# The causal mask of a hybrid decoder layer: added on VectorE instead of multiplied in on TensorE, with a re-set table of waits

## The chip, the cores and the metric

The kernel runs on one core of a Trainium2 chip. The metric is the device time of one execution in microseconds (us), the median of several; lower is better. TensorE (PE) multiplies matrices into the eight PSUM banks, VectorE (DVE) and ScalarE (ACT) work on 128 partitions at a time and can read and write banks, GpSimd (POOL) does a few small operations, and DMA queues bring the weights from memory. Each engine takes its instructions in the order in which the program issues them, and waits at an instruction whose inputs are not there.

## What is computed

One decoder layer on 256 tokens of width 1024. An input projection feeds two groups of heads: eight heads of softmax attention (width 64, rotary on 16 dimensions) and four heads of retention (rotary queries and keys, a fixed decay table in place of a softmax, normalising and a gate). Both go through an output projection; then come cross-attention into 256 memory rows and a gated feed-forward part, each with normalising before and after and a residual.

The attention blocks are 256 keys long and the sequence has 256 tokens, so only a query's own block counts, and the reference comes down to causal attention:

```python
    scale = dh ** -0.5
    ...
        s_own = jnp.einsum('bhqd,bhld->bhql', qb, k_own).astype(jnp.float32) * scale
        own_pos = cur * L + key_offsets
        s_own = jnp.where(own_pos[None, :] <= q_pos[:, None], s_own, NEG_INF)
        ...
        p = jax.nn.softmax(logits, axis=-1)
```

The mask is what the change concerns: keys later than the query get -1e30 before the softmax.

## The kernel before

**The main line.** All large products are cut into 257 steps (`steps`), each of six or so products of 128x128 weights on 512 columns; PE runs them one after the other. Weights arrive as raw 128x1024 blocks and are split into a high and a low part, one ScalarE copy (L196) and one VectorE subtraction (L197) each; three products then stand in for one of full precision. Steps 0 to 16 make q and k, 17 to 24 the retention's q and k, 25 to 32 its values, 33 to 40 its gate, 41 to 48 the attention's values, and 49 to 64 the output projection. Step 49 starts with the gated retention rows of the first 128 tokens, step 50 with those of the last 128.

**The side work.** Everything else (rotations, softmax, retention, normalising) is written as generators. A generator does some work, yields a number of steps, and is resumed after that many steps (`spawn`, `run_side`); inside a step the side work is issued after the step's products. The numbers come from the table `WAIT`, so the table sets the order of the instructions on every engine. A generator that yields 0 goes on in the same step; one that is spawned by another generator is resumed at the next step at the earliest.

**The splits.** At the end of a step at most one weight is split. Weight `q` may be split at step `i` if `q <= 2 + WAIT["pace"] * 0.01 * i`, if a buffer is free, and if the step had no side work or the weight is near its use (six weights ahead).

**Attention.** `moba_qk` scales q or k (L241), turns it (L278 to L283), and after `rope_*` steps transposes it through the one bank of pool C (L287, L288). `mq` is the wait ahead of q's. `moba_units` then runs three softmax units through `moba_unit` and `softmax_unit`: m00 (first 128 queries, all heads, 128 keys), m10 and m11 (last 128 queries, 256 keys, four heads each). A unit fills two of the four banks of pool S with scores (`fill`, L352); the mask is added by a product of an identity with the mask table: after the scores with bfloat16 operands in m00 and m10 (L356), ahead of them with float32r operands in m11 (L345). Then VectorE takes the maxima (L302), ScalarE the exponentials (L312), VectorE normalises (L315, L317), and after `nm_*` steps PE transposes the weights (L325) into two banks of pool S, which ScalarE (L330) and VectorE (L332) copy out. `u1` and `u2` are the steps between units. In m11, `fill` also issues the first half of the retention scores (`ret_scores`: L423 on PE, L430 on VectorE), and the second half is a generator of its own, `rs` steps later.

**Around it.** `ret_qk` turns and transposes the retention's q and k (L400 to L411). `mem_stats` takes the mean square of the memory rows, their power -1/2 on GpSimd (L219), and `mrow` steps later `row_rms` spreads them over a row through the bank of pool C (L248, L249). `ret_out` and `ret_gate` (`gate0`, `gate1`; transposes L466, split L235, L236) and `moba_pv` (`pv1`; L388) make the operands of the output projection. `x_stats` makes the four operands of the mask products (L1034 to L1037).

By the table before, the steps after which these are issued are: m00's scores 20 and transposes 25; m10's scores 28 and transposes 34; m11's scores and the first retention scores 36, its normalising 40 and transposes 46; retention rotation transposes 27 and 33; the memory row 30; the gates' transposes 42 and 46; the attention-value product 50.

Of the kernel before, what the change touches and what calls it, by code (L numbers as in the profile page):

```python
# [8 lines left out]
F32R = mybir.dt.float32r  # L9
BF16 = mybir.dt.bfloat16  # L10
AF = mybir.ActivationFunctionType
ALU = mybir.AluOpType
AX = mybir.AxisListType

P = 128
# [21 lines left out]

WAIT = {
    "cpb0": 2, "cpb1": 1, "cpv0": 7, "cpv1": 1, "cu0": 3, "cu1": 4, "ex_c0": 2, "ex_c1": 1, "ex_m00": 0,
    "ex_m10": 0, "ex_m11": 4, "f0_0": 8, "f0_1": 5, "g_add": 1, "g_silu": 5, "gate0": 3, "gate1": 6,  # L40
    "gp1": 5, "gp2": 0, "k_add": 0, "k_hl": 3, "lag": 2, "ret": 9, "low": 6, "mq": 0, "mrow": 4, "ms": 21, "mst": 5,
# [5 lines left out]
}  # L47
# [4 lines left out]
C_ID, C_MASK, C_MCOS, C_MSIN, C_RCOS, C_RSIN, C_DEC, C_END = 0, 128, 256, 288, 320, 448, 576, 1600  # L52
# [3 lines left out]
def tile_hybrid_layer(  # L56
# [14 lines left out]
    nc = tc.nc  # L71
    ctx.enter_context(tc.manual_schedule())

    cpool = ctx.enter_context(tc.tile_pool(name="cpool", bufs=1))
# [12 lines left out]
    def tok(t):  # L87
        return slice(t * P, (t + 1) * P)
# [4 lines left out]
    def small(name):  # L93
        return sm.tile([P, 8], F32, tag="sm", name=name)
# [10 lines left out]
    cst = cpool.tile([P, C_DEC], F32, tag="cst", name="cst")  # L105
    xg = cpool.tile([P, 288], F32, tag="xg", name="xg")
    gp = xg[:, 0:32].rearrange("p (g k) -> p g k", g=4)
    x_sb = cpool.tile([P, 2, D], F32, tag="x", name="x_sb")
    identb = cpool.tile([P, P], BF16, tag="identb", name="identb")
    maskb = cpool.tile([P, P], BF16, tag="maskb", name="maskb")  # L110
    identr = cpool.tile([P, P], F32R, tag="identr", name="identr")
    maskr = cpool.tile([P, P], F32R, tag="maskr", name="maskr")
    junk = cpool.tile([P, D], BF16, tag="junk", name="junk")
    mhalf = cpool.tile([P, 8], F32, tag="mhalf", name="mhalf")
    ident = cst[:, C_ID:C_ID + P]
# [5 lines left out]
    T = {}  # L121
# [3 lines left out]
    def need(*keys):  # L125

        missing = [k for k in keys if k not in emitted]
        assert not missing, missing
# [83 lines left out]
    def inv_rms(key, ss0, ss1=None, n=1):  # L212
        v = small(f"v_{key}")
        if ss1 is None:
            nc.vector.tensor_scalar(v[:, :n], ss0, EPS, None, op0=ALU.add)
        else:
            nc.vector.tensor_scalar(v[:, :n], ss0, ss1, EPS, op0=ALU.add, op1=ALU.add)
        r = cpool.tile([P, 8], F32, tag=f"r_{key}", name=f"r_{key}")
        nc.gpsimd.tensor_tensor(out=r[:, :n], in0=v[:, :n], in1=mhalf[:, :n], op=ALU.pow)  # L219
        rstd[key] = r  # L220
        return r

    def mean_square(dst, src, n):
        nc.scalar.activation(junk[:, :n], src, AF.Square, scale=1.0 / 32.0, accum_out=dst)
# [31 lines left out]
    def spawn(gen, wait=0):  # L256
        active.append([step_no[0] + wait, gen])
# [76 lines left out]
    def moba_unit(t, g):  # L334
        keys = P * (t + 1)
        n = D // keys
        hn = n // 2

        def fill(s):

            need(f"q{t}", *[f"k{u}" for u in range(t + 1)])

            ahead = g == 1
            for e in range(2) if ahead else ():
                nc.tensor.matmul(s[e].rearrange("p (h k) -> p h k", h=hn)[:, :, keys - P:keys], identr,  # L345
                                 maskr[:, None, :].to_broadcast([P, hn, P]), start=True, stop=False,
                                 skip_group_check=True)
            for i in range(hn):
                j = g * hn + i
                for e in range(2):  # L350
                    rows = slice(64 * e, 64 * e + 64)
                    nc.tensor.matmul(s[e][:, i * keys:(i + 1) * keys], T["qT"][rows, j, tok(t)],  # L352
                                     T["kT"][rows, j, 0:keys], start=(i == 0 and not ahead),
                                     stop=(ahead and i == hn - 1), skip_group_check=True)
            for e in range(2) if not ahead else ():
                nc.tensor.matmul(s[e].rearrange("p (h k) -> p h k", h=hn)[:, :, keys - P:keys], identb,  # L356
                                 maskb[:, None, :].to_broadcast([P, hn, P]), start=False, stop=True,
                                 skip_group_check=True)
            if ahead:
                scores = ret_scores()  # L360
                spawn(scores, next(scores))
            yield 0

        return softmax_unit(f"m{t}{g}", n, keys, 0.125, fill)

    def moba_units():
# [47 lines left out]
    def ret_scores():  # L414

        need("rqk0", "rqk1")
        for kb in range(2):
            n = P * (2 - kb)
            s = [accS(f"rs{kb}{e}") for e in range(2)]
            for j in range(2):  # L420
                for e in range(2):
                    rows = slice(64 * e, 64 * e + 64)
                    nc.tensor.matmul(s[e][:, j * n:(j + 1) * n], T["rkT"][rows, j, tok(kb)],  # L423
                                     T["rqT"][rows, j, kb * P:256], start=True, stop=True)
            for e in range(2):
                if kb == 0 or e == 0:
                    buf = tmp2k(f"ra{kb}{e}")
                a = buf[:, kb * e * 256:kb * e * 256 + 2 * n].rearrange("p (j i) -> p j i", j=2)
                T[f"ra{kb}{e}"] = a
                nc.vector.tensor_tensor(out=a, in0=s[e][:, 0:2 * n].rearrange("p (j i) -> p j i", j=2),  # L430
                                        in1=T["decay"].rearrange("p (j e) i -> p e j i", e=2)[:, e, :, 0:n], op=ALU.mult)
            if kb == 0:
                yield WAIT["rs"]
# [478 lines left out]
    for what in USE:  # L912
# [4 lines left out]
        elif what[0] == "d":  # L917
            k = int(what[1:])
# [17 lines left out]
    for q, item in enumerate(items):  # L936
        if item[0] == "w":
            continue
        kind, w, g, home, part, plus = item[:6]
# [91 lines left out]
        yield 0  # L1031

    def x_stats():
        nc.vector.tensor_copy(identb, ident)  # L1034
        nc.vector.tensor_copy(maskb, cst[:, C_MASK:C_MASK + P])
        nc.vector.tensor_copy(identr, ident)
        nc.vector.tensor_copy(maskr, cst[:, C_MASK:C_MASK + P])  # L1037
        for t in range(2):
            ss = small(f"ss_x{t}")
            mean_square(ss[:, 0:1], x_sb[:, t, :], D)  # L1040
            inv_rms(f"x{t}", ss[:, 0:1])
        yield 0
# [25 lines left out]
    x_split(2, 3)  # L1068
    opening = {4: lambda: x_split(4, 5), 7: lambda: x_split(6, 7)}
    late = {WAIT["xd"]: x_load, WAIT["xs"]: x_stats, WAIT["ms"]: mem_stats}  # L1070
    pending_split = list(range(2, NQ))

    accs, downs = {}, {}
    for i, s in enumerate(steps):
# [17 lines left out]
        if s[0] == "first":  # L1092
# [3 lines left out]
            h = hls[q][:, :, c * 512:(c + 1) * 512]  # L1096
# [6 lines left out]
        elif s[0] == "col":  # L1103
# [4 lines left out]
            h = hls[q].rearrange("p s (k n) -> p s k n", k=2)  # L1108
            for kk in range(2):
                k = 2 * kp + kk  # L1110
# [9 lines left out]
        elif s[0] == "row":  # L1120
# [13 lines left out]
            for k, w in ops:  # L1134
                begin = half == 0 and (k, w) == ops[0]
                end = half == 1 and (k, w) == ops[-1]
                if w:
                    nc.tensor.matmul(acc, hls[q][:, 0, k * P:(k + 1) * P], T[f"{st}_k"][:, k, :], start=begin, stop=end,  # L1138
                                     skip_group_check=True)
                else:  # L1140
                    nc.tensor.matmul(acc[:, 0:256], hls[q][:, 1, k * P:(k + 1) * P], T[st][:, 0, k, :], start=begin,  # L1141
                                     stop=end, skip_group_check=True)
            if half == 1:
                spawn(done(nt, acc))
        elif s[0] == "down":
            _, q, t, j, kk, halves = s
# [17 lines left out]
        elif s[0] == "seven":  # L1164
            _, q, g, m, part, name, begin = s
# [3 lines left out]
            h = hls[q].rearrange("p s (k n) -> p s k n", k=2)  # L1169
            for kk in range(2):  # L1170
                xh, xl = token_operand(m, 2 * part + kk)
                end = part == 1 and kk == 1
                for n, (a, w) in enumerate(((xh, 0), (xh, 1), (xl, 0))):
                    nc.tensor.matmul(acc, a, h[:, w, kk, :], start=begin and kk == 0 and n == 0, stop=end and n == 2,  # L1174
                                     skip_group_check=True)
# [132 lines left out]
```

## Time and profile before

| | |
|---|---|
| median of 3 runs | 398.38 us (398.0 to 398.8) |
| profiled execution | 400.7 us |
| its span, first to last instruction | 398.9 us |
| PE busy | 390.0 us, 98% |
| VectorE busy | 320.3 us, 80% |
| ScalarE busy | 257.6 us, 65% |
| GpSimd busy | 33.4 us, 8% |
| granted TensorE clock | 0.998 |

Rows of a timeline read: start in us, duration in us, engine, line, operation, output<-inputs, output shape and type<-input shape and type, how many were merged; in brackets the idle time of the engine ahead of it and what ended it. PE is the products, PEld the loading of their weights. A row in the chain of waits has start, duration, engine and line. The ends of products are modelled, so the starts of the next ones are the better mark. In a table of stretches each engine has its busy time and its number of instructions; the last three columns are the granted clock, the share of the DMA engines and GB/s.

### The profile page before, as it was taken

The page shows a single profiled execution, that of the slowest core. Times are in us where ns is not written, and L with a number is a line of the kernel's source. Part 1 is how long each engine was busy: PE and PEld are TensorE (multiplying, and loading weights), DVE is VectorE, ACT ScalarE, POOL GpSimd, SP SyncE. Part 2 cuts the span into 40 slices and gives each one's busy share as a digit, 9 for nine tenths or more (in the row PEclk, how much of TensorE's full clock was granted, in tenths as well). Part 3 has the DMA queues.
Part 4 walks back from the last instruction along what each step waited for, and adds up shares of the span by engine and source line. Part 5 has one row for each costly group of instructions (what it writes and reads, how often), then busy time and mean ns, then how long its engine had stood idle before and what let it go on. Part 6 is the DMA issues. An engine that isn't in the chain of part 4 may idle for free.

```text
span 398.9 us, 5470 instructions
## 1 busy us (share of the span) xinstructions
PE 390.0 (98%) x1969; PEld 323.9 (81%) x1969; DVE 320.3 (80%) x447; ACT 257.6 (65%) x431; POOL 33.4 (8%) x53
## 2 busy tenths in 40 slices
PE   7999999999999999999999999999999999999993
PEld 3888887888888888888888888888887888888882
DVE  3876877586869987677576699999899899999964
ACT  4885973964757865494547766766748685656741
POOL 0010020200011000000001001013113103101000
PEclk9999999999999999999999999999999999999999
DMA  8998837367547676607271459778939878954102
GB/s 275 414 354 268 300 118 252 107 187 287 168 152 223 200 215 204 214 4 235 79 263 55 158 193 358 242 157 315 278 72 279 241 242 175 372 191 71 38 0 105
DMA packets 23067, 80.36 MB, mean 201 GB/s; under 512 B 2560, under 2 KB 3200, under 8 KB 23040
## 3 DMA queue, kind: packets, MB, share of 16 engines
q1 hardware_dynamic: 18288, 62.97, 45.7%
q0 software_dynamic: 4608, 16.78, 17.1%
q8 instruction: 15, 0.25, 0.3%
q10 hardware_dynamic: 144, 0.26, 0.2%
q14 instruction: 12, 0.10, 0.1%
HBM read 78.95 MB, written 1.05 MB: 201 GB/s over the span
## 4 chain that ended last, share of the span: by engine, by line
PE 78%; issue 7%; DMA 7%; DVE 4%; ACT 1%; POOL 1%; SPq 0%; DVEq 0%; ACTq 0%; POOLq 0%
PE acc L1114 11%; PE acc L1116 11%; PE acc L1115 11%; PE acc L1138 7%; PE x L1174 7%; PE acc L1141 4%; PE down L1161 3%; PE down L1159 3%; PE down L1160 3%; PE y L1174 3%; DMA sum_qv<-in_weights_dram 3%; DVE hl L197 2%; PE acc L1102 2%; DMA sum_ret<-in_weights_dram 2%; DMA xr<-in_gx_dram 2%
## 5 line engine op out<-in xcount | busy, mean ns | idle before, releaser
L197 DVE TENSOR_TENSOR hl<-raw,hl 128x1024 fp32r<-128x1024 f32 (+1 forms) x102 | 119.3, 1189 | 16.9 <-ACT hl L196 16.8
L196 ACT ACTIVATE hl<-raw 128x1024 fp32r<-128x1024 f32 (+1 forms) x102 | 102.5, 1031 | 1.1 <-DMA raw<-in_weights_dram 0.9
L196 ACT ACTIVATE hl<-sum_qv 128x1024 fp32r<-128x1024 f32 x22 | 23.0, 1057 | 16.5 <-DVE sum_qv L203 12.9
L1114 PE MATMUL acc<-hl,xT 128*128 128x512 f32 x80 | 32.9, 411 | 0.0
L1159 PE MATMUL down<-hl,fT 128*128 128x512 f32 x80 | 31.3, 392 | 0.0
L1116 PE MATMUL acc<-hl,xT 128*128 128x512 f32 x80 | 31.3, 391 | 0.0
L1115 PE MATMUL acc<-hl,xT 128*128 128x512 f32 x80 | 31.2, 391 | 0.0
L1161 PE MATMUL down<-hl,fT 128*128 128x512 f32 x80 | 31.2, 390 | 0.0
L1160 PE MATMUL down<-hl,fT 128*128 128x512 f32 x80 | 31.1, 389 | 0.0
L197 DVE TENSOR_TENSOR hl<-sum_kT,hl 128x1024 fp32r<-128x1024 f32 x24 | 29.1, 1221 | 1.4 <-ACT hl L196 1.2
L196 ACT ACTIVATE hl<-sum_kT 128x1024 fp32r<-128x1024 f32 x24 | 24.8, 1051 | 5.5 <-DVE sum_kT L203 3.5
L197 DVE TENSOR_TENSOR hl<-sum_qv,hl 128x1024 fp32r<-128x1024 f32 x22 | 26.7, 1219 | 1.9 <-ACT hl L196 1.9
L1174 PE MATMUL x<-hl,comb 128*128 128x512 f32 x96 | 23.6, 392 | 0.4 <-DVE hl L197 0.4
L1174 PE MATMUL x<-hl,x2T 128*128 128x512 f32 x96 | 23.1, 392 | 0.0
L1174 PE MATMUL y<-hl,comb 128*128 128x512 f32 x96 | 23.1, 389 | 0.0
L1174 PEld LDWEIGHTS x<-hl,comb 128*128 128x128 f32 x96 | 17.9, 188 | 4.8 <-DVE hl L197 1.1
L1174 PEld LDWEIGHTS y<-hl,comb 128*128 128x128 f32 x96 | 18.0, 188 | 3.8
L1174 PEld LDWEIGHTS x<-hl,x2T 128*128 128x128 f32 x96 | 17.8, 188 | 3.6
L1161 PEld LDWEIGHTS down<-hl,fT 128*128 128x128 f32 x80 | 15.0, 188 | 3.3 <-DVE fT L664 0.2
L1116 PEld LDWEIGHTS acc<-hl,xT 128*128 128x128 f32 x80 | 15.0, 188 | 3.3
L1114 PEld LDWEIGHTS acc<-hl,xT 128*128 128x128 f32 x80 | 15.0, 188 | 3.2 <-issue 0.3
L1160 PEld LDWEIGHTS down<-hl,fT 128*128 128x128 f32 x80 | 15.0, 188 | 3.1
(260 smaller groups left out, 861.8 us busy)
## 6 DMA issues: line engine op xcount, KB each, us to landing
raw<-in_weights_dram SPq DMA_DIRECT2D x98, 512.0 KB, 4.8
sum_kT<-in_weights_dram POOLq DMA_DIRECT2D x14, 512.0 KB, 6.9
sum_qv<-in_weights_dram POOLq DMA_DIRECT2D x10, 512.0 KB, 5.7
sum_ret<-in_weights_dram POOLq DMA_DIRECT2D x8, 512.0 KB, 4.8
gpost<-in_gpost_dram SPq DMA_DIRECT2D x3, 512.0 KB, 5.2
x_sb<-in_x_dram SPq DMA_DIRECT2D x2, 512.0 KB, 8.1
memn<-in_mem_dram SPq DMA_DIRECT2D x2, 512.0 KB, 8.0
mr<-in_memT_dram SPq DMA_DIRECT2D x2, 512.0 KB, 7.4
```

Source lines behind the costliest of these rows:

```text
L196: nc.scalar.activation(h[:, 0, n], raw[:, n], AF.Copy)
L197: nc.vector.tensor_tensor(out=h[:, 1, n], in0=raw[:, n], in1=h[:, 0, n].bitcast(F32), op=ALU.subtract)
L1102: nc.tensor.matmul(accs[(c, t)], T["xT"][:, hx, q, tok(t)], h[:, hw, :], start=begin, stop=False)
L1114: nc.tensor.matmul(acc, xh, h[:, 0, kk, :], start=(first and kk == 0), stop=False)
L1115: nc.tensor.matmul(acc, xh, h[:, 1, kk, :], start=False, stop=False)
L1116: nc.tensor.matmul(acc, xl, h[:, 0, kk, :], start=False, stop=(last and kk == 1))
L1138: nc.tensor.matmul(acc, hls[q][:, 0, k * P:(k + 1) * P], T[f"{st}_k"][:, k, :], start=begin, stop=end, skip_group_check=True)
L1141: nc.tensor.matmul(acc[:, 0:256], hls[q][:, 1, k * P:(k + 1) * P], T[st][:, 0, k, :], start=begin, stop=end, skip_group_check=True)
L1159: nc.tensor.matmul(acc, fh, wh, start=first, stop=False, skip_group_check=True)
L1160: nc.tensor.matmul(acc, fh, wl, start=False, stop=False, skip_group_check=True)
L1161: nc.tensor.matmul(acc, fl, wh, start=False, stop=last, skip_group_check=True)
L1174: nc.tensor.matmul(acc, a, h[:, w, kk, :], start=begin and kk == 0 and n == 0, stop=end and n == 2, skip_group_check=True)
```

## The change

The mask products go, and after the scores of each unit VectorE adds the mask table to the diagonal 128 keys of every head, in the bank, one instruction for each of the unit's two banks. m11 has the same order as the others. The four operand copies in `x_stats` and their tiles go. In the table of waits ten entries change:

| entry | before | after |
|---|---|---|
| `mq`, ahead of q's rotation | 0 | 3 |
| `rope_q0`, `rope_q1`, rotation of q to its transposes | 5, 8 | 2, 5 |
| `u2`, from m10's transposes to m11's scores | 2 | 0 |
| `nm_m11`, normalising to transposes | 6 | 4 |
| `rs`, between the halves of the retention scores | 0 | 1 |
| `gate0`, `gate1` | 3, 6 | 7, 8 |
| `pv1`, ahead of the attention-value product | 2 | 3 |
| `pace`, of the weight splits | 58 | 59 |

```diff
@@ moba_unit, fill
-            ahead = g == 1
-            for e in range(2) if ahead else ():
-                nc.tensor.matmul(s[e].rearrange("p (h k) -> p h k", h=hn)[:, :, keys - P:keys], identr,
-                                 maskr[:, None, :].to_broadcast([P, hn, P]), start=True, stop=False,
-                                 skip_group_check=True)
             for i in range(hn):
...
                     nc.tensor.matmul(s[e][:, i * keys:(i + 1) * keys], T["qT"][rows, j, tok(t)],
-                                     T["kT"][rows, j, 0:keys], start=(i == 0 and not ahead),
-                                     stop=(ahead and i == hn - 1), skip_group_check=True)
-            for e in range(2) if not ahead else ():
-                nc.tensor.matmul(s[e].rearrange("p (h k) -> p h k", h=hn)[:, :, keys - P:keys], identb,
-                                 maskb[:, None, :].to_broadcast([P, hn, P]), start=False, stop=True,
-                                 skip_group_check=True)
-            if ahead:
+                                     T["kT"][rows, j, 0:keys], start=(i == 0), stop=(i == hn - 1), skip_group_check=True)
+            for e in range(2):
+                diag = s[e].rearrange("p (h k) -> p h k", h=hn)[:, :, keys - P:keys]
+                nc.vector.tensor_tensor(out=diag, in0=diag, in1=cst[:, None, C_MASK:C_MASK + P].to_broadcast([P, hn, P]),
+                                        op=ALU.add)
+            if g == 1:
                 scores = ret_scores()
                 spawn(scores, next(scores))
@@ x_stats
-        nc.vector.tensor_copy(identb, ident)
-        nc.vector.tensor_copy(maskb, cst[:, C_MASK:C_MASK + P])
-        nc.vector.tensor_copy(identr, ident)
-        nc.vector.tensor_copy(maskr, cst[:, C_MASK:C_MASK + P])
```

By the new table, m11's scores and the first retention scores are issued after step 34, in the step of m10's transposes; m11's normalising after step 38 and its transposes after 42; the gates' transposes after steps 46 and 48; the attention-value product after 51. The other steps named above stay.

More of the change, by code (lines that the diff above doesn't have):

```diff
@@ L39 @@
     "cpb0": 2, "cpb1": 1, "cpv0": 7, "cpv1": 1, "cu0": 3, "cu1": 4, "ex_c0": 2, "ex_c1": 1, "ex_m00": 0,
-    "ex_m10": 0, "ex_m11": 4, "f0_0": 8, "f0_1": 5, "g_add": 1, "g_silu": 5, "gate0": 3, "gate1": 6,
-    "gp1": 5, "gp2": 0, "k_add": 0, "k_hl": 3, "lag": 2, "ret": 9, "low": 6, "mq": 0, "mrow": 4, "ms": 21, "mst": 5,
[3 rows of a table removed]
+    "ex_m10": 0, "ex_m11": 4, "f0_0": 8, "f0_1": 5, "g_add": 1, "g_silu": 5, "gate0": 7, "gate1": 8,
+    "gp1": 5, "gp2": 0, "k_add": 0, "k_hl": 3, "lag": 2, "ret": 9, "low": 6, "mq": 3, "mrow": 4, "ms": 21, "mst": 5,
[3 rows of a table added]
     "xa_mix0": 8, "xa_mix1": 4, "near": 18, "now": 5, "sum": 3, "ts": 2, "ts0": 1, "ts1": 3, "s_silu": 4, "s_t0": 4, "s_mul": 1, "s_t1": 1, "xd": 3, "xh_cross0": 1, "xh_cross1": 1, "xh_mix0": 2, "xh_mix1": 2, "xn0": 2, "xn1": 2, "hold0": 1, "hold": 2, "hold_low": 3,
@@ L108, in tile_hybrid_layer @@
     x_sb = cpool.tile([P, 2, D], F32, tag="x", name="x_sb")
[L109 to L112, printed above, removed]
     junk = cpool.tile([P, D], BF16, tag="junk", name="junk")
```

6 rows, old and new, of the table WAIT are left out of this document.

## The prediction

> **What bounds the kernel now.** I read the page first, then the table of waits for the tensor engine (PE), then the busy time by stretches, then the timeline from 22 to 96 us engine by engine, and last the chain of waits. The page gives the span, the waits give what PE ever waited for:
>
> ```profile
> span 398.9 us, 5470 instructions
> ```
> ```profile
> PE acc L1102 <- ACT hl L196: 1.4, 1, 1.4
> ...
> PE x L1174 <- DVE hl L197: 0.4, 1, 0.4
> ```
>
> PE waits at the very start and once late, and nowhere between, so a microsecond of PE work taken out or a microsecond of new PE waiting moves the end by about itself. The profiled execution took 400.7 us, 1.8 of it around the span and 2.3 more than the median of the runs, 398.38 us; I work in differences inside the span and put them on the median. The change sits in the attention part, and there the two helper engines are not idle (columns: PE, PEld, DVE, ACT, POOL busy us):
>
> ```profile
> 40.00:50.00 10.00, 10.00 (x54) 8.10 (x54) 8.84 (x14) 9.25 (x19) 0.00 (x0) 1.00 0.82 297
> 50.00:60.00 10.00, 10.00 (x53) 8.00 (x52) 7.24 (x12) 7.45 (x19) 2.04 (x2) 1.00 0.40 120
> 60.00:70.00 10.00, 10.00 (x61) 7.91 (x60) 7.27 (x11) 3.90 (x10) 0.00 (x0) 1.00 0.69 247
> ```
>
> From 40 to 50 us DVE is at 8.84 and ACT at 9.25 of 10: the work that leaves PE goes to the engine with the least room, in its fullest stretch. The question is what PE will wait for there.
>
> **What PE loses.** The first unit (m00) has two mask products of 512 columns, the others (m10, m11) two of 256 each.
>
> ```profile
> 36.04 0.60 PE L356 MATMUL s_m<-maskb,identb 128*128 128x512 bf16 x2
> ...
> 36.71 0.40 PE L1115 MATMUL acc<-hl,xT 128*128 128x512 f32 x1
> ...
> 36.95 0.39 PE L1116 MATMUL acc<-hl,xT 128*128 128x512 f32 x1
> ```
> ```profile
> 50.87 0.39 PE L356 MATMUL s_m<-maskb,identb 128*128 128x256 bf16 x2
> ...
> 51.33 0.40 PE L1115 MATMUL acc<-hl,xT 128*128 128x512 f32 x1
> ```
> ```profile
> 358.96 2.72 PE x L1174 x12
> ```
>
> A product starts every 0.23 us (12 in 2.72 us, so one step of six takes 1.36 us). The one that starts at 36.71 has one before it that needed until then from 36.48, so m00's masks held PE from 36.04 to 36.48: 0.44 us. The same reading at m10, 51.33 less 0.23 less 50.87, gives 0.23 us, and m11's pair has the same width: 0.23 us. PE gains 0.90 us.
>
> **What VectorE gets.** Six additions on the score banks in place of that. No row of before writes a bank from VectorE; the nearest read one and write SBUF, of the same shapes:
>
> ```profile
> 65.99 1.29 DVE L430 TENSOR_TENSOR ra<-rs,rvd 128x512 f32<-128x512 f32 x2 [1.76 <-PE rs L423]
> ...
> 68.58 0.75 DVE L430 TENSOR_TENSOR ra<-rs,rvd 128x256 f32<-128x256 f32 x2
> ...
> 75.38 0.69 DVE L453 TENSOR_TENSOR on<-ro,r_ro 128x512 f32<-128x512 f32 x1 [1.13 <-POOL r_ro L219]
> ```
>
> One of 512 lasts 0.69 us, two take 1.29, so one occupies the queue for 0.60 us, with 0.09 of overlap; two of 256 take 0.75, so 0.33 each, and about 0.34 with the handover. m00 gets 1.20 us, m10 and m11 0.68 each, 2.56 in all. If in place on a bank gains nothing from overlap, they are 0.79 and 0.42 each; if it were half as dear, 0.30 and 0.17. I take the L430 rows, since they have the same operation, shapes and source, and keep both ends. [...] No run here has yet shown the write into a bank.
>
> **The four copies that go** (L1034 to L1037) win nothing on the path:
>
> ```profile
> 23.01 0.23 DVE L1034 CAST identb<-cst 128x128 bf16<-128x128 f32 x1 [1.63 <-DMA cst<-in_consts_dram]
> ...
> 23.42 0.22 DVE L1037 CAST maskr<-cst 128x128 fp32r<-128x128 f32 x1
> ...
> 24.48 1.23 DVE L197 TENSOR_TENSOR hl<-raw,hl 128x1024 fp32r<-128x1024 f32 x1 [0.72 <-ACT hl L196]
> ```
>
> Four from 23.01 to 23.64 us, and behind them VectorE sits idle 0.72 us for ScalarE anyway. If that cover were gone they would give 0.6 us to VectorE, not to PE.
>
> **First wait: m00's transposes.** The whole chain of a unit is serial: scores, (now: additions), maxima, exponentials, normalising, transposes.
>
> ```profile
> 36.47 1.29 DVE L302 TENSOR_REDUCE mx_m<-s_m 128x4 f32<-128x512 f32 x2
> ...
> 38.05 0.37 ACT L312 ACTIVATE p_m<-s_m,nb_m 128x128 f32<-128x128 f32 x1 [2.85 <-DVE nb_m L306]
> ...
> 41.23 1.23 DVE L317 TENSOR_TENSOR p_m<-p_m,rs_m 128x1024 f32<-128x1024 f32 x1
> ```
> ```profile
> 43.78 1.04 PE L325 MATMUL pt_m<-cst,p_m 128*128 128x128 f32 x8
> ```
>
> The maxima start when VectorE comes free from a weight split (36.47), not when the scores are there, so the additions take that place and all behind them comes 1.20 us later: normalised at 41.23 + 1.23 + 1.20 = 43.66. PE, 0.44 us early, wants them at 43.34. Wait 0.32; PE stands at -0.12 against before.
>
> **How far the helpers fall back.** The 1.20 us of VectorE are not made good before the next unit: from the row at 41.23 above to that at 51.88 below there are 16, with no gap between them. m10's additions make it 1.88 us:
>
> ```profile
> 46.68 0.60 ACT L288 ACTIVATE kr<-c_k 128x512 f32<-128x512 f32 x1 [0.72 <-PE c_k L287]
> ```
> ```profile
> 51.88 1.28 DVE L302 TENSOR_REDUCE mx_m<-s_m 128x2 f32<-128x512 f32 x2
> ```
> ```profile
> 53.53 0.48 ACT L312 ACTIVATE p_m<-s_m,nb_m 128x256 f32<-128x256 f32 x1 [2.55 <-DVE nb_m L306]
> ```
>
> ScalarE has 0.72 us to spare at 46.68 and then waits 2.55 us for VectorE's maxima, so its exponentials start at 53.53 + 1.88 = 55.41. From there its rows touch each other (the last of those I use starts at 57.51, and VectorE's split at 61.27 below still waits for one), so everything it does for PE there is 1.88 us late.
>
> **Second wait: the memory row.** The change leaves the row's own wait (mrow) at 4; only what stands before it gets longer.
>
> ```profile
> 50.85 2.04 POOL L219 TENSOR_TENSOR r_mem<-v_mem,mhalf 128x1 f32<-128x1 f32 x2 [25.92 <-DVE v_mem L215]
> ```
> ```profile
> 53.61 0.36 PEld L248 LDWEIGHTS c_R_mem<-cst,r_mem 128*128 128x128 f32 x2
> ```
>
> GpSimd's two powers follow VectorE's queue, so they end at 52.89 + 1.20 = 54.09. PE, at -0.12 and less m10's 0.23, wants them at 53.26. Wait 0.83; PE at +0.48.
>
> **Third wait: the retention rotation's transposes** need bank C back from the memory row's copy (L249).
>
> ```profile
> 56.30 0.39 ACT L249 ACTIVATE R_mem<-c_R_mem 128x256 f32<-128x256 f32 x1
> 56.56 1.08 ACT L196 ACTIVATE hl<-raw 128x1024 fp32r<-128x1024 f32 x1
> 57.51 1.28 ACT L241 ACTIVATE rvd<-acc,r_x 128x512 f32<-128x512 f32 x2
> ```
> ```profile
> 57.92 0.58 PEld L409 LDWEIGHTS c_r<-cst,nat_r 128*128 128x128 f32 x4
> 58.47 0.19 PEld L1114 LDWEIGHTS acc<-hl,xT 128*128 128x128 f32 x1
> ```
>
> The pace decides what else stands before that copy. Weight q may be split from step (q - 2)/pace on: for q = 19 that is 17/0.58 = 29.3, so step 30 and behind the row's copy; with 0.59 it is 28.8, so step 29 and ahead of it. The split that starts at 56.56 holds ScalarE until 57.51, 0.95 us. The copy then ends at 56.30 + 1.88 + 0.95 + 0.39 = 59.52; PE wants its bank at 57.92 + 0.48 = 58.40. Wait 1.12; PE at +1.60. The values' first copy ends at 57.51 + 0.69 + 1.88 = 60.08, and the product that takes its bank starts at 58.47 + 1.60 = 60.07: no wait, and none to spare.
>
> **Fourth wait: two units in one step.** Before, m10's transposes are issued after step 34, and m11's scores with the first retention scores two steps later (u2 = 2). With u2 = 0 all of it is issued after step 34. The four S banks go round: m10's transposes fill two, m11's scores the two that m10's scores held, and the retention scores the first two again, which the copies of the transposed weights must have emptied, one by ScalarE, one by VectorE (L332).
>
> ```profile
> 59.98 1.03 PE L325 MATMUL pt_m<-cst,p_m 128*128 128x128 f32 x8
> ...
> 63.96 1.14 PE L352 MATMUL s_m<-kr,qv 64*128 64x256 f32 x8
> 64.92 1.03 PE L423 MATMUL rs<-kr 64*128 64x256 f32 x8
> ```
> ```profile
> 61.27 1.23 DVE L197 TENSOR_TENSOR hl<-raw,hl 128x1024 fp32r<-128x1024 f32 x1 [0.27 <-ACT hl L196]
> 62.41 0.68 DVE L332 COPY ptT_m<-pt_m 128x512 f32<-128x512 f32 x1
> ```
>
> VectorE's copy stands behind the split of weight 21, which waits for ScalarE; weight 21 is still split at step 33 (19/0.59 = 32.2). So the copy ends at 63.09 + 1.88 = 64.97. PE reaches the transposes at 59.98 + 1.60 = 61.58, is through them 0.90 us later, through m11's scores after another 0.96 (64.92 less 63.96), and the second retention score wants its bank at about 63.55. Wait 1.42. In before the distance of two steps, 2.72 us, hid this copy; that is the cover which the change takes away.
>
> **The rest of the waits that change.** m11's normalising and transposes come 4 steps earlier (u2 and nm_m11), in a stretch where ScalarE idles; q's two rotations start 3 steps later, and their transposes stay where they were (0 + 5 against 3 + 2); rs 0 or 1 resumes at the next step either way; no DMA is issued in another order by these. The later gate transposes and attention-value product come nearer to the products that use them.
>
> ```profile
> 84.46 0.47 PEld L466 LDWEIGHTS c_ro<-cst,on 128*128 128x128 f32 x4
> ```
> ```profile
> 86.57 0.68 DVE L236 TENSOR_TENSOR mixT<-c_ro,mixT 128x512 fp32r<-128x512 f32 x1
> ```
>
> The second gate's operand took 2.8 us from 84.46 to 87.25. Issued after step 48, it has step 49 and a third of step 50, 1.8 us. I price it at 0 because VectorE no longer has m11's copy before it there (it does that 4 steps earlier); if it had the same queue the price is 1.0 us. With pace 0.59 some splits come a step earlier; none is late in before, and the raw loads follow them.
>
> **Sum.** Waits 0.32 + 0.83 + 1.12 + 1.42 = 3.69 us, less 0.90 of PE work: +2.79. A second way: the retention scores run at 64.97 instead of 64.92, and two steps (2.72) that stood before them are still to be done: +2.77. In this form the first three waits do not count one by one; the end is set by VectorE's copy. With additions at half price the fall-back is 0.94 us and this gives +1.83, at the dear end (2.42) +3.31. Nothing behind gives it back: later stages are started by PE's own progress, and the late wait of 0.4 us is the most that could vanish. Forecast: 398.38 + 2.8 = 401.2 us.
>
> **Rivals.** *Faster:* the helpers' fall-back stays inside the slack, nobody waits and PE keeps its 0.90: 397.5 us. For it: PE waits nowhere in 36 to 90 us of before, and ScalarE has a long idle stretch:
>
> ```profile
> 68.77 0.48 ACT L312 ACTIVATE p_m<-s_m,nb_m 128x256 f32<-128x256 f32 x1 [6.10 <-DVE nb_m L306]
> ```
>
> Against it: those 6.10 us lie behind the four waits. It decides at VectorE's copy: it would have to end by 61.30 (64.92 less 2.72 less 0.90), 1.79 us before it ends today, so the splits ahead of it would have to stand behind it. *Another bank:* if the retention scores find empty banks, the fourth wait goes: 1.60 less 0.23, +1.37, 399.8 us. For it is only that I infer the banks' order; against it, before already shows the second retention scores waiting for the first to be emptied, so there are no spare ones. *Nothing:* the waits and the 0.90 us cancel, 398.4 us; this needs the third and fourth waits to be a third of what I have. That the change does not do what it says: the words speak of a longer wait for the memory row, which the diff does not have; a row a step later would only hand its 0.83 us on to the third wait, so the time is the same.
>
> **How the numbers follow.** The forecast, +1.8 to +3.4, 0.58; the bank rival and its neighbours, +0.3 to +1.7, 0.15; nothing 0.10; faster 0.17. Faster and slower by over 0.2%, 0.8 us, is what the runs of before (398.0 to 398.8) let one tell. So slower 0.73, same 0.10, faster 0.17. The range goes from 398.0, which takes in the case of nothing, to 402.8: the dear end, +3.3, with 1.0 for the gate. The forecast's own range is 400.2 to 401.8.
>
> **What would show it.** In the profile of the changed kernel: additions of about 0.69 and 0.42 us on s_m; PE waiting for p_m (0.3), r_mem (0.8), R_mem (1.1) and, longest, the retention scores for VectorE's L332 copy; ScalarE's second exponentials 1.9 us later against VectorE's maxima. No wait on VectorE in the PE table between 40 and 70 us, or additions under 0.3 us, would make it wrong.

## The result and the profile after

| | before | after |
|---|---|---|
| median | 398.38 us (398.0 to 398.8, 6 runs) | 401.37 us (401.04 to 401.47, 6 runs) |
| ratio | | 1.0074, 95% interval 1.0061 to 1.0087 |
| profiled execution | 400.7 us | 401.3 us |
| its span | 398.9 us | 399.5 us |

The changed kernel is 3.0 us slower; 401.2 was forecast. The two spans differ by only 0.6 us, and the reason has to be cleared first. Most of it lies in the first microseconds, ahead of anything that the change touches. The second piece of x that is split (`xr`; the first is in `xg`) landed late in the profile of before. ScalarE's first row for it there, in a second profile of the same kernel (the fourth experiment), and after:

```profile
8.18 0.51 ACT L229 ACTIVATE xT<-xr,xg 128x256 fp32r<-128x256 f32 x1 [2.63 <-DMA xr<-in_gx_dram]
```
```profile
6.37 0.51 ACT L229 ACTIVATE xT<-xr,xg 128x256 fp32r<-128x256 f32 x1 [0.95 <-DMA xr<-in_gx_dram]
```
```profile
6.27 0.51 ACT L225 ACTIVATE xT<-xr,xg 128x256 fp32r<-128x256 f32 x1 [0.85 <-DMA xr<-in_gx_dram]
```

So the starts differ, and rows of the two kernels are compared from a common point. I take the loading of k's first transposes (after step 19) as the start and that of the attention-value product as the end. Before, in the first and in the second profile, then after:

```profile
32.80 0.59 PEld L287 LDWEIGHTS c_k<-cst,nat_k 128*128 128x128 f32 x4
...
90.57 2.60 PEld L388 LDWEIGHTS o_m<-ptT_m,qv 128*64 128x64 f32 x48 [0.35 <-issue]
```
```profile
30.97 0.59 PEld L287 LDWEIGHTS c_k<-cst,nat_k 128*128 128x128 f32 x4
...
88.79 2.60 PEld L388 LDWEIGHTS o_m<-ptT_m,qv 128*64 128x64 f32 x48 [0.35 <-issue]
```
```profile
31.18 0.59 PEld L283 LDWEIGHTS c_k<-cst,nat_k 128*128 128x128 f32 x4
...
93.35 2.60 PEld L377 LDWEIGHTS o_m<-ptT_m,qv 128*64 128x64 f32 x48 [0.35 <-issue]
```

This stretch lasts 57.77 and 57.82 us in the two profiles of before, though their spans are 398.9 and 396.2. After, it lasts 62.17 us, of which one step of 1.36 us is there because the attention-value product is issued one step later: 60.81, or 3.0 us more. The whole loss is in the stretch: from its end to the end of the span there are 306.1 us after and 307.4 in the second profile of before, and the 1.3 between them is that step. After is 1.62 us ahead of the first profile of before at its start. That profile also has 0.9 us more than the second one behind the stretch (308.3), most of it at one late weight split that PE waited for:

```profile
PEld x L1174 <- DVE hl L197: 1.1, 2, 0.8
```

So 3.0 us of loss, less 1.6 ahead of the stretch and some 0.8 behind it, leave the 0.6 by which the spans differ. I call this stretch "the stretch" below and always take out that step where it applies. (A row of waits like the one above reads: who waited for whom, us in total, how often, the longest. The changed kernel is shorter, so its line numbers are smaller: L328 is L332 of before, L412 is L423, L398 is L409, L245 is L249, L237 is L241.)

Busy time in the attention part after (columns PE, PEld, DVE, ACT, POOL):

```profile
50.00:60.00 10.00, 8.99 (x42) 6.71 (x40) 7.73 (x14) 6.34 (x16) 2.04 (x2) 1.00 0.40 114
60.00:70.00 10.00, 9.32 (x54) 6.76 (x53) 5.98 (x11) 5.04 (x14) 0.00 (x0) 1.00 0.55 200
```

PE, at 10.00 of 10 in the same rows of before, now misses 1.01 us in the first and 0.68 in the second. The timeline shows what held it. First the helpers: the additions, the maxima behind them, the normalising, the copy that counts most; then the powers and m10's exponentials:

```profile
34.76 1.29 DVE L346 TENSOR_TENSOR s_m<-s_m,cst 128x512 f32<-128x512 f32 x2
35.96 1.28 DVE L298 TENSOR_REDUCE mx_m<-s_m 128x4 f32<-128x512 f32 x2
...
40.70 1.23 DVE L313 TENSOR_TENSOR p_m<-p_m,rs_m 128x1024 f32<-128x1024 f32 x1
...
51.35 0.76 DVE L346 TENSOR_TENSOR s_m<-s_m,cst 128x256 f32<-128x256 f32 x2
52.01 1.28 DVE L298 TENSOR_REDUCE mx_m<-s_m 128x2 f32<-128x512 f32 x2
...
61.38 1.23 DVE L193 TENSOR_TENSOR hl<-raw,hl 128x1024 fp32r<-128x1024 f32 x1 [0.84 <-ACT hl L192]
62.53 0.68 DVE L328 COPY ptT_m<-pt_m 128x512 f32<-128x512 f32 x1
```
```profile
50.32 2.04 POOL L215 TENSOR_TENSOR r_mem<-v_mem,mhalf 128x1 f32<-128x1 f32 x2 [27.19 <-DVE v_mem L211]
```
```profile
53.66 0.47 ACT L308 ACTIVATE p_m<-s_m,nb_m 128x256 f32<-128x256 f32 x1 [4.06 <-DVE nb_m L302]
```

And PE's side of it, the weight loads that came late, with the idle time ahead of each in brackets:

```profile
42.04 0.86 PEld L321 LDWEIGHTS pt_m<-cst,p_m 128*128 128x128 f32 x8 [0.44 <-ACT qv L284]
...
52.41 0.13 PEld L244 LDWEIGHTS c_R_mem<-cst,r_mem 128*128 128x128 f32 x1 [0.38 <-POOL r_mem L215]
...
57.81 0.42 PEld L398 LDWEIGHTS c_r<-cst,nat_r 128*128 128x128 f32 x4 [1.36 <-ACT R_mem L245]
...
61.89 0.29 PEld L412 LDWEIGHTS rs<-kr 64*128 64x128 f32 x2 [0.30 <-ACT ptT_m L326]
63.27 0.73 PEld L412 LDWEIGHTS rs<-kr 64*128 64x128 f32 x6 [1.08 <-DVE ptT_m L328]
...
90.85 0.19 PEld L1101 LDWEIGHTS acc<-hl,mixT 128*128 128x128 f32 x1 [0.34 <-DVE mixT L232]
```

These are the four waits of the forecast, in their order, and the gate's as a fifth.

### The profile page after: what moved, and what is told of

Same layout as the page of the kernel before. It is cut to its first block, busy times and chain, and to the rows that moved or that the text cites. A ratio compares the mean times of both kernels' runs of the same rounds, so it can differ in the third digit from the quotient of the medians.

```text
span 399.5 us, 5467 instructions
## 1 busy us (share of the span) xinstructions
PE 390.5 (98%) x1963; PEld 323.3 (81%) x1963; DVE 322.5 (81%) x449; ACT 257.6 (64%) x431; POOL 33.3 (8%) x53
## 4 chain that ended last, share of the span: by engine, by line
PE 89%; DVE 4%; ACT 3%; issue 1%; DMA 1%; DVEq 0%; ACTq 0%
PE x L1159 11%; PE acc L1099 10%; PE acc L1101 10%; PE acc L1100 10%; PE acc L1123 9%; PE y L1159 5%; PE down L1146 5%; PE down L1144 5%; PE down L1145 5%; PE acc L1126 5%; PE acc L1087 3%; PE z L1159 3%; DVE hl L193 2%; ACT hl L192 1%; ACT p_m L308 1%
```

## The experiments

The theory: each helper engine works in the order of issue, the additions push everything behind them back, and PE pays where it next needs something from far down those queues; the table moves such needs nearer. Two rivals: the additions cost what they last wherever they stand, or the table alone does the harm. Times are medians with their ratio to before, measured beside each (the ratio is not exactly the quotient of the two medians).

| run | median, us | ratio (95% interval) | stretch: from, to | against 57.82 |
|---|---|---|---|---|
| after | 401.37 | 1.0074 (1.0061 to 1.0087) | 31.18, 93.35 | +2.99 |
| e1, additions only | 399.74 | 1.0031 (1.0018 to 1.0044) | 30.93, 90.02 | +1.27 |
| e2, table only | 400.05 | 1.0045 (1.0030 to 1.0061) | 31.69, 92.10 | +1.23 |
| e3, pace only | 398.61 | 1.0004 (0.9994 to 1.0014) | 31.02, 88.83 | -0.01 |
| e4, before again | 398.0, one run | | 30.97, 88.79 | 0 |
| e5, scores apart again | 399.98 | 1.0038 (1.0024 to 1.0052) | 31.79, 92.49 | +1.52 |
| e6, copy on ScalarE | 400.96 | 1.0052 (1.0035 to 1.0068) | 32.24, 93.54 | +2.12 |
| e7, added twice | 404.08 | 1.0128 (1.0103 to 1.0152) | 31.65, 96.37 | +5.54 |
| e8, pace 58 | 402.05 | 1.0077 (1.0052 to 1.0101) | 31.24, 93.40 | +2.98 |
| e9, joined only | 399.48 | 1.0032 (1.0018 to 1.0045) | 31.42, 90.25 | +1.01 |
| e10, m10 and m11 | 398.46 | 1.0001 (0.9992 to 1.0010) | 31.26, 89.28 | +0.20 |
| e11, m11 alone | 398.42 | 0.9995 (0.9984 to 1.0007) | 31.90, 89.53 | -0.19 |

In after, e2 and e5 to e8 the step of 1.36 us is taken out. The times differ from run to run by several tenths, the stretch by a few hundredths (57.77, 57.82 and, in e3, 57.81), so the small terms are read from the stretch and the times are held beside it.

### e1: the additions with the table of before

From after:

```diff
-"gate0": 7, "gate1": 8, "mq": 3, "nm_m11": 4, "pace": 59, "pv1": 3, "rope_q0": 2, "rope_q1": 5, "rs": 1, "u2": 0
+"gate0": 3, "gate1": 6, "mq": 0, "nm_m11": 6, "pace": 58, "pv1": 2, "rope_q0": 5, "rope_q1": 8, "rs": 0, "u2": 2
```

> The additions on VectorE with the table of waits of before. Queue theory: PE gains 0.90 us of mask products; the helpers fall back by 1.20 and then 0.68 us more. PE waits 0.3 for the first normalised weights, 0.4 to 0.8 for the memory row's power, and then for the copy of the first retention values (it had 0.27 us to spare), together 2.0 to 2.4; the copy of m10's transposed weights stays hidden behind two steps. So 1.1 to 1.5 us above before, about 399.7, and additions of 0.69 and 0.42 us. Rival, the additions' own 2.6 us all land on the path and the table is harmless: about 3 us above before, as with the whole change. Rival, the table does all the harm: 0.9 us below before.

Measured: 399.74, the stretch 1.27 us longer. The waits of e1:

```profile
PEld acc L1099 <- ACT rvd L237: 1.1, 1, 1.1
...
PEld pt_m L321 <- ACT qv L284: 0.5, 1, 0.5
PEld c_r L398 <- ACT R_mem L245: 0.5, 1, 0.5
```

As the queue theory had it, down to the wait for the first retention values; a second, smaller one for the memory row's copy stands beside it. PE doesn't wait for VectorE's copy of m10's weights (L328) here. Both rivals miss, one by 1.7 us and one in sign.

### e2: the table with the mask products

From before:

```diff
-"gate0": 3, "gate1": 6, "mq": 0, "nm_m11": 6, "pace": 58, "pv1": 2, "rope_q0": 5, "rope_q1": 8, "rs": 0, "u2": 2
+"gate0": 7, "gate1": 8, "mq": 3, "nm_m11": 4, "pace": 59, "pv1": 3, "rope_q0": 2, "rope_q1": 5, "rs": 1, "u2": 0
```

> The mask products of before with the table of waits of after. Queue theory: nothing falls back, but m11's scores and the first retention scores are issued in the step of m10's transposes, and the retention scores wait for VectorE's copy of the transposed weights, which ends at 63.1 in the profile of before: 0.7 to 0.9 us above before, 399.1 to 399.3, with one wait of PE in the retention scores. Rival, the additions do all the harm: no change. Rival, the table does all the harm: 3 to 4 us above before.

Measured: 400.05, the stretch 1.23 us longer. The queue theory named the wait but was 0.4 short; the time says 1.6, with an interval down to 1.2. The waits of e2 show the other part, which is the gate's, at the output projection's first products:

```profile
PEld rs L423 <- DVE ptT_m L332: 0.8, 1, 0.8
...
PEld acc L1116 <- DVE mixT L236: 0.3, 1, 0.3
```

So neither half is harmless; they are about equal. They add up to 2.50 us and not to the 2.99 of both together, because the copy's delay by the additions is hidden in e1 and not once the table is there. From before to after, VectorE's copy of m10's weights, counted from the stretch's start, ends 1.75 us later (61.25 - 30.97 in e4 against 63.21 - 31.18), and from e2 to after the stretch grows by 1.76 us.

### e3: the pace

From before:

```diff
-"pace": 58
+"pace": 59
```

> Before with the pace at 59 and nothing else. Queue theory, followed further along the queues than in the prediction: with 59 weight 23 is split at step 36 and not 37, so its subtraction stands on VectorE ahead of the second half of the retention's decay products (step 37), and it waits for a ScalarE copy that stands behind m11's exponentials; PE then waits for those decay products in the retention output: about 2.7 us above before, 401. Rival, the one I held in the prediction (a step more or less of the splits costs nothing by itself): within 0.3 us of before.

Measured: nothing (1.0004, stretch -0.01). The order on VectorE did change as foreseen; the second half of the decay products (128x256) stands behind a split that waits for ScalarE:

```profile
69.94 1.23 DVE L197 TENSOR_TENSOR hl<-raw,hl 128x1024 fp32r<-128x1024 f32 x1 [3.01 <-ACT hl L196]
71.08 0.75 DVE L430 TENSOR_TENSOR ra<-rs,rvd 128x256 f32<-128x256 f32 x2
```

In e4 the same products start at 66.80, so they come 4.2 us later from the stretch's start, and PE does not wait: the retention output of the first 128 tokens reads only the first half (`ra0`), and the one that reads the second comes a step later. I had charged the first one with both. So a delay of 4.2 us in a queue cost nothing here (-0.01 in the stretch), because its reader was later still; one has to look at which instruction the reader is.

### e4: before, profiled again

The kernel before, with no edit.

> Before unchanged, for a second profile. The first one took 2.3 us more than the median of the runs. If that lies in how the first loads landed (the first product of the second weight waited 1.4 us for its split there, not in the profile of after), this profile shows it gone and a span near 397; if the kernel itself always does so, it is there again.

The late load is gone, as shown above, and the span is 2.7 us shorter (396.2). Of this, 1.8 us lie ahead of the stretch (32.80 against 30.97); the other 0.9 lies behind it, where PE's late wait at L1174 is gone too. Both belonged to that execution.

### e5: m11's scores two steps behind again

From after:

```diff
-"u2": 0, "nm_m11": 4
+"u2": 2, "nm_m11": 6
```

> The whole change, but m11's scores are again two steps behind m10's transposes and its own transposes six steps behind its normalising, as before. By the prediction's fourth wait alone: the copy of m10's weights is hidden again, so 1.4 us less than after, about 400. By the queues followed further: with the pace at 59 the split of weight 23 then stands on VectorE ahead of the second half of the decay products, behind m11's exponentials, and the retention output waits 2.9 us for it: 1.2 to 1.5 us more than after, about 402.8.

Measured: 399.98, the stretch 1.47 us shorter than after. That is the prediction's fourth wait (1.42), alone; the further-going guess falls with e3's. In e5 the retention scores wait only for their own decay products, as before:

```profile
PEld rs L412 <- DVE ra L419: 0.4, 1, 0.4
```

### e6: m10's copies both on ScalarE

From after:

```diff
-            elif b == 0:
-                nc.scalar.activation(pt[:, 0:4, :], src, AF.Copy)
+            elif b == 0 or key == "m10":
+                nc.scalar.activation(pt[:, 4 * b:4 * b + 4, :], src, AF.Copy)
```

> The whole change, but both copies of m10's transposed weights are made by ScalarE (none by VectorE). Queue theory: in the profile of after ScalarE ends its copy at 61.84 and then has nothing to do until 66.8, so the second would end at about 62.4 instead of VectorE's 63.2; the retention scores' wait of 1.08 falls to about 0.3: 0.6 to 0.9 us below after, about 400.6. Rival, the length is set by how late the helpers are as a whole and not by this copy: no change against after.

Measured: the stretch is 0.87 us shorter than after, and the wait for VectorE's copy is replaced by two short ones for ScalarE:

```profile
PEld rs L412 <- ACT ptT_m L326: 0.5, 2, 0.3
```

The time, 400.96 against before's 398.59 beside it, is 2.4 us over, against after's 3.0; the two intervals overlap, so the time alone would not prove it. The copy's place in VectorE's queue is what sets the length.

### e7: every addition twice

From after:

```diff
+                for _ in range(2):
                     nc.vector.tensor_tensor(out=diag, in0=diag, in1=cst[...], op=ALU.add)
```

> The whole change with every addition made twice (the masked scores are then lower by the mask once more, which changes no weight). Queue theory: the fall-back grows from 1.9 to 3.8 us, the end follows VectorE's copy of m10's weights one to one: 1.7 to 2.1 us above after, about 403.3. Rival, the fall-back is partly taken up by idle time of the helpers: under 1 us above after. Rival, the additions don't matter at all: no change against after.

Measured: 404.08, the stretch 2.55 us longer than after, more than the 1.7 to 2.1 of the expectation. The second additions are dearer than the first. The two of after, on two banks, follow each other at 0.60 us. Of the 2.76 us of the first row below, less 0.69 for the last addition and 0.60 from bank to bank, 1.47 are left for the two steps that stay on a bank: an estimate of 0.73 each, more than the 0.69 that one addition lasts, so no overlap is left there:

```profile
35.23 2.76 DVE L347 TENSOR_TENSOR s_m<-s_m,cst 128x512 f32<-128x512 f32 x4
...
53.30 1.69 DVE L347 TENSOR_TENSOR s_m<-s_m,cst 128x256 f32<-128x256 f32 x4
...
65.41 0.68 DVE L328 COPY ptT_m<-pt_m 128x512 f32<-128x512 f32 x1
```

Four of 512 take 2.76 us where two took 1.29, four of 256 take 1.69 where two took 0.76: 1.47 + 0.93 = 2.40 us more in m00 and m10. The copy, counted from the stretch's start, ends 2.41 us later than in after (66.09 - 31.65 against 63.21 - 31.18), and the stretch grows by 2.55. So the time for which the additions hold VectorE's queue goes on to PE nearly one to one, and no idle time of the helpers takes it up. It doesn't show which wait sets the end: PE's wait for that copy is no longer than in after (1.08), and the new time is in the waits ahead of it, for m00's weights (0.44 in after) and for the memory row's copy (1.36):

```profile
PEld c_r L399 <- ACT R_mem L245: 2.3, 1, 2.3
PEld pt_m L321 <- ACT qv L284: 1.9, 1, 1.9
PEld rs L413 <- DVE ptT_m L328: 1.1, 1, 1.1
```

### e8: after with the pace of before

From after:

```diff
-"pace": 59
+"pace": 58
```

> The whole change with the pace left at 58. Queue theory: the split of weight 19 stands behind the memory row's copy again, so the wait of the retention rotation's transposes falls from 1.36 to about 0.3, but the first retention values' copy is as late as it was and the product that takes its bank waits about 1.0 instead; the fourth wait is the same. 0 to 0.3 us below after. Rival, the third wait counts by itself: 1.0 us below after.

Measured: the stretch is the same to 0.01 us (the time, 402.05 with a ratio of 1.0077, is not told apart from after's 1.0074). The waits changed places as expected; the rotation's transposes wait 0.4 instead of 1.4, and the product that takes the retention values' bank 1.1:

```profile
PEld acc L1099 <- ACT rvd L237: 1.1, 1, 1.1
```

### e9: two units in one step, nothing else

From before:

```diff
-"u2": 2, "nm_m11": 6
+"u2": 0, "nm_m11": 4
```

> Before with m11's scores in the step of m10's transposes (u2 = 0) and m11's transposes four steps behind its normalising (nm_m11 = 4); mask products, gates and pace of before. Queue theory: only the wait of the retention scores for VectorE's copy is left of what the table alone did; 0.7 to 1.0 us more than before in the stretch from k's transposes to the attention-value product, and no wait at the output projection's first products. Rival, the gates and the pace make up a good part of what the table alone costs (1.25 us in that stretch): 0.3 or less here.

Measured: 1.01 us in the stretch, with one new wait, and the output projection's is not there:

```profile
PEld rs L423 <- DVE ptT_m L332: 0.8, 1, 0.8
```

So of what the table alone costs, 1.0 is this step. The rest, 0.2 us, is most likely the gates', whose wait in e2 is 0.3; `mq`, `rope_q*`, `rs` and the gates had no run of their own.

### e10: additions in m10 and m11 alone

From before:

```diff
-            ahead = g == 1
+            ahead = False
...
-                                     stop=(ahead and i == hn - 1), skip_group_check=True)
-            for e in range(2) if not ahead else ():
+                                     stop=(t == 1 and i == hn - 1), skip_group_check=True)
+            for e in range(2) if t == 0 else ():
                 nc.tensor.matmul(..., identb, maskb[...], start=False, stop=True, skip_group_check=True)
-            if ahead:
+            for e in range(2) if t == 1 else ():
+                diag = s[e].rearrange("p (h k) -> p h k", h=hn)[:, :, keys - P:keys]
+                nc.vector.tensor_tensor(out=diag, in0=diag, in1=cst[...], op=ALU.add)
+            if g == 1:
```

> Before, with the additions in m10 and m11 alone; m00 keeps its mask products, and the table is that of before. Queue theory: m00's 1.20 us of fall-back are gone, m10's 0.68 stay; PE gains 0.46, waits for neither m00's weights nor the memory row, and waits about 0.5 to 0.7 for the copy of the first retention values: 0 to 0.3 us above before. Rival, every addition costs what it lasts: 1.3 us above before.

Measured: 398.46, the stretch 0.20 us longer, with one new wait:

```profile
PEld acc L1118 <- ACT rvd L241: 0.5, 1, 0.5
```

Four of the six additions, 1.4 us of VectorE, cost 0.2 us net, which the time can't tell from nothing (0.9992 to 1.0010); the two of m00 are the dear ones (1.27 with them, 0.20 without).

### e11: additions in m11 alone

The edit of e10, with other conditions:

```diff
-                                     stop=(t == 1 and i == hn - 1), skip_group_check=True)
-            for e in range(2) if t == 0 else ():
+                                     stop=(g == 1 and i == hn - 1), skip_group_check=True)
+            for e in range(2) if g == 0 else ():
...
-            for e in range(2) if t == 1 else ():
+            for e in range(2) if g == 1 else ():
```

> Before, with the additions in m11 alone, whose chain has room; m00 and m10 keep their mask products, and the table is that of before. Queue theory: PE gains 0.23 to 0.33 us of products and waits nowhere new: 0.2 to 0.4 us below before in the stretch from k's transposes to the attention-value product, and about as much in the time, which the runs may not tell from no change. Rival, any addition in a score bank costs PE: 0.2 us or more above before.

Measured: the stretch is 0.19 us shorter, just short of the 0.2 to 0.4 expected and about the width of the two products taken out (0.23), and PE waits nowhere new. The time (0.9995, interval 0.9984 to 1.0007) can't tell that from no change. This is the best that the idea gave here; no run beat before clear of its noise.

## Why the prediction was right

**PE's gain (0.90 us).** Not measured by itself as a whole; m11's part is confirmed by e11 (0.19 against 0.23). The whole fits: the six idle times of PE's loads shown above add up to 3.90 us, less 0.90 that is 3.00, and the stretch has 2.99.

**The additions' price.** Right: 1.29 us for two of 512, 0.76 for two of 256, as the rows of the decay products said (1.29 and 0.75). In the queue they hold 1.20 (34.76 to 35.96) and 0.66 us (51.35 to 52.01); that the result goes into a bank and not into SBUF cost nothing extra. The dear end of the range was mis-sized: two of 512 without any overlap are 0.69 each by the row, not 0.79, so the four additions of m00 and m10 are 2.22 us (2 x 0.69 and 2 x 0.42) and not 2.42, and +3.31 should have been +3.11.

**The first wait.** Forecast 0.32, measured 0.44. The row names ScalarE's copy of q as the releaser, but that ended at 41.86, and the normalised weights at 41.93, 0.11 ahead of the load.

**The fall-back.** Forecast 1.88 us at m10's exponentials; 53.66 against 53.53 less 1.62 is 1.75.

**The second wait.** Forecast 0.83, measured 0.38: I let PE wait for both powers, but the row's two transposes are separate instructions, and only the second waits for the second power. It made no difference to the sum, because the next wait is set by ScalarE and took the rest:

**The third wait.** Forecast 1.12, measured 1.36. Put on the time of the first profile of before, the transposes started at 57.81 + 1.62 = 59.43, and 59.52 was forecast. By e8 the pace, to which I gave 0.95 us of it, only decides whether PE waits for the memory row's copy or, as long, for the retention values'. So the 0.95 is no cost of the pace, as the sum has it: without it the forecast would have had the same delay in the next wait.

**The fourth wait.** Forecast 1.42, measured 0.30 + 1.08. VectorE's copy ended at 63.21 + 1.62 = 64.83, and 64.97 was forecast. e5 takes this wait away and finds 1.47, e6 shortens it, e9 makes it alone (1.01), and from e2 to after the stretch grows by 1.76, with the copy 1.75 later than in before. In e7 the wait stays as it is, because PE and the copy both come later.

**The gate.** Priced at 0, bounded by 1.0; measured 0.34 us after (0.3 in e2). My reason for 0 looked at VectorE alone. ScalarE's queue after has the two copies of the attention's values and a split ahead of the gate's operand:

```profile
87.30 0.69 ACT L237 ACTIVATE qv<-acc,r_x 128x512 f32<-128x512 f32 x1 [0.79 <-PE acc L1101]
87.89 1.05 ACT L192 ACTIVATE hl<-raw 128x1024 fp32r<-128x1024 f32 x1
88.84 0.68 ACT L237 ACTIVATE qv<-acc,r_x 128x512 f32<-128x512 f32 x1
89.41 0.59 ACT L231 ACTIVATE mixT<-c_ro 128x512 fp32r<-128x512 f32 x1
```

The transposes were loaded at 88.26, and the copy could start only at 89.41.

**The sum.** Forecast +2.79 from the waits and +2.77 from the copy's end; measured +2.99 in the stretch and in the time. The 0.22 beyond the second way's sum are about the gate's 0.34 less the 0.14 by which VectorE's copy ended earlier than forecast; that these two partly cancel is luck. The second way of adding up was the better one, since it goes by the last wait alone and doesn't depend on how the earlier ones share the delay.

**The rivals.** That PE keeps its gain holds only for m11 (e11). That the retention scores find other banks is out (e9). What I said of the sum's halves, +1.83 with additions at half price, wasn't tried; more time on VectorE was (e7).

## What to carry to other kernels

VectorE was 80% busy on average and had nothing to spare where work was moved to it: before, its rows follow one another without a wait from 41.23 to 51.88 us. Follow the moved work down its new engine's queue to the first thing that the bound engine needs from behind it: the price here was that item's lateness (the copy 1.75 us later, the stretch 1.76 longer from e2 to after) and not the work's own time (1.29, 0.76 and 0.75 us in the three units). With the table of before, and net of the products that they replace, the additions cost 1.1 us in the first unit (e1 less e10), 0.4 in the next (e10 less e11) and were a gain of 0.2 in the last (e11). And before two pieces of work are issued closer together, ask which buffers the second takes from the first, and where in which queue their emptying stands.

## What was not expected of the hardware

Additions in place on a PSUM bank were no dearer than products read from a bank and written to SBUF (1.29 us for two of 128x512 both ways), but a second one on the same bank had, by the estimate under e7, no overlap with the first: four in pairs took 2.76 us. And one execution of the same kernel had one piece of x 1.8 us later (ScalarE's row for it at 8.18 instead of 6.37 us) and never made that up; with a late weight split far behind, its span was 2.7 us longer.
